# A hybrid decoder on one core: adaLN products one to a softmax step, and the softmax normalisation of five heads on ScalarE

## The chip, the cores and the metric

The kernel runs on one core of a Trainium2 chip. The metric is device time in microseconds (us) for one execution. The engines are named as in the profile: PE is TensorE's matmuls and PEld its weight loads, DVE is VectorE, ACT is ScalarE, POOL is GpSimd, and SP is the engine that issues most DMAs. A name followed by q (SPq) is the engine's instruction queue.

## The reference

The program is a two-layer decoder on 512 tokens of 1024 channels, all in float32. Layer 0 has attention, layer 1 a gated delta rule, and each has a SwiGLU FFN. What matters here is layer 0: a modulation vector computed from the condition `c`, and eight softmax heads ("moba") beside eight stick-breaking heads.

```python
cond = jax.nn.silu(c)
mod = (cond @ ada_w[layer] + ada_b[layer])          # 6 x 1024 numbers: six vectors
shift_m, scale_m, gate_m, shift_f, scale_f, gate_f = jnp.split(mod, 6, axis=-1)
h = rmsnorm(x, norm_mix_g) * (1 + scale_m) + shift_m
p = softmax(concat([s_sel, s_own]))                 # softmax heads; for 512 keys: causal
oa = p @ v                                          # then the stick-breaking heads, and
x = x + gate_m * (concat([oa, ob]) @ w_out)         # the output projection
h = rmsnorm(x, norm_ffn_g) * (1 + scale_f) + shift_f
x = x + gate_f * swiglu(h)
```

## The kernel before

Float32 accuracy is had by splitting each operand of a matmul into a high and a low part (`split`, L249 on ACT for the high part, L254 on DVE for the low part) and multiplying three times. Every engine runs its own instructions strictly in the order in which they stand in its queue; a scheduler with a cost model of its own makes these orders when the program is built, from the data dependencies and from `tc.issue_after`, which holds an instruction back until another one stands in the queue.

**The adaLN products.** Each of the 6 x 8 column blocks of the modulation needs the product of a 128x1024 block of `ada_w` with `cond`, summed along the row. `ada` (L206) issues a 512 KB DMA on SP's queue (L209) into the tile `aw` and then one DVE instruction (L214). The pool holds two `aw` tiles, so the third DMA can start only when the first product is done. The first two of the six vectors are needed before attention and are computed there; the last is left to the FFN. The 24 products of vectors 2, 3 and 4 fall in the attention stage.

**The softmax heads.** The heads run in four pairs; `moba` does one softmax head in four steps of 128 queries (i = 0 to 3) with 128 to 512 keys each, followed by `stick` for a stick-breaking head. A step is a chain: PE makes the scores `s` in a single PSUM bank (L744 to L747), DVE takes the row maximum (L759), ACT the exponential with its row sum (L761), DVE the reciprocal of the sum (L762) and the product of `p` with it (L763, "normalisation"), PE transposes `p` (L767), ACT and DVE split the result. Between these chains the scheduler places the `stick` work (`z`, `u`, `ssh`, `ssl`, `sq`) and the projections of the next pair (`mm` <- `hh`, `wh`), so that PE always has something.

**Where the 24 products stand.** `ADA = (0, 6, 6, 6, 6, 0, 0, 0)` puts six of them behind the reciprocal of the last step of each of the second to fifth heads (L814 to L817). In the output projection, `between` would take those left over, which are none.

The weights of the output projection (`raw` <- attn_out) are loaded on SP's queue (L292) between and behind these DMAs, and then the residual `x` (L153).

Of the kernel before, what the change touches and what calls it, by code (L numbers as in the profile page):

```python
# [12 lines left out]
AF = mybir.ActivationFunctionType  # L13
OP = mybir.AluOpType
# [53 lines left out]
OG, NG = (6, 8), 18  # L68
GS = 4
ROT = 2  # L70
AENG = "v"
ADA = (0, 6, 6, 6, 6, 0, 0, 0)
NSPLIT = 4
NFIRST = 2
NFIRST_GDN = 2
# [55 lines left out]
def build(nc, tc, I, O):  # L131
    V, G, A, PE = nc.vector, nc.gpsimd, nc.scalar, nc.tensor
    from contextlib import ExitStack
    ctx = ExitStack()
    with ctx:
# [38 lines left out]
        apool = actx.enter_context(tc.tile_pool(name="apool", bufs=1))  # L174
        cond = apool.tile([128, D], F32, name="cond")
# [27 lines left out]

        mod = const.tile([128, 96], F32, name="mod")

        def ada(layer, comp, chunk, pool=apool, bufs=2, eng="v"):  # L206
            j = layer * 48 + comp * 8 + chunk
            w = pool.tile([128, D], F32, name="aw", tag="aw", bufs=bufs)
            nc.sync.dma_start(w, I["ada_w"][j])  # L209
            if eng == "g":  # L210
                ins = G.tensor_tensor(w, w, cond, op=OP.mult)
                A.activation(w, w, AF.Copy, accum_out=mod[:, j:j + 1])
                return ins
            return V.tensor_tensor_reduce(w, w, cond, 1.0, 0.0, OP.mult, OP.add, mod[:, j:j + 1])  # L214

        fin = const.tile([128, 96], F32, name="fin")
# [318 lines left out]
def attention(e, x0ctx):  # L535
    nc, tc, V, G, A, PE, I = e.nc, e.tc, e.V, e.G, e.A, e.PE, e.I
    from contextlib import ExitStack
    with ExitStack() as ctx:
# [73 lines left out]
        with e.psum_pool("start") as sp:  # L612
            pq = [sp.tile([128, T], F32, name=f"pq{i}") if i < 1 else e.mm_tile() for i in range(4)]
            pv = [sp.tile([128, T], F32, name=f"pv{i}") for i in range(4)]
            with e.pool("rtmp") as tmp:
                for k in range(KC):
# [7 lines left out]
                    ins = e.norm_h(FULL, 0, 0, 1, hs, (k,))  # L624
# [3 lines left out]
                    a, z = k == 0, k == KC - 1  # L628
# [111 lines left out]
        def qk3(ps, k, ks, q, qs, at, mask):  # L740

            kh, kl = k
            qh, ql = q
            PE.matmul(ps, kh[:, ks], qh[:, qs], start=True, stop=False)  # L744
            PE.matmul(ps, kh[:, ks], ql[:, qs], start=False, stop=False)
            PE.matmul(ps[:, at], e.identb, mask, start=False, stop=False)
            steps[-1].append(PE.matmul(ps, kl[:, ks], qh[:, qs], start=False, stop=True).ins)  # L747

        def moba(pair, h, q, k):

            ph = work.tile([128, 1920], F32R, name="ph", tag="ph", bufs=1)
            pl = work.tile([128, 1920], F32R, name="pl", tag="pl", bufs=1)
            for i in range(4):
                n = 128 * (i + 1)
                qs = slice(i * 128, n)
                s = psum.tile([128, T], F32, name="s", tag="s", bufs=1)
                qk3(s[:, :n], q[h], qs, k, slice(0, n), qs, causal)
                st = work.tile([128, 3], F32, name="st", tag="st", bufs=4)
                V.tensor_reduce(st[:, 0:1], s[:, :n], AX.X, OP.max, negate=True)  # L759
                p = work.tile([128, T], F32, name="p", tag="p", bufs=2)  # L760
                A.activation(p[:, :n], s[:, :n], AF.Exp, bias=st[:, 0:1], accum_out=st[:, 1:2])  # L761
                ins = V.reciprocal(st[:, 2:3], st[:, 1:2])  # L762
                V.tensor_scalar(p[:, :n], p[:, :n], st[:, 2:3], None, op0=OP.mult)  # L763
                pt = psum.tile([128, T], F32, name="pt", tag="pt", bufs=1)
                for j in range(i + 1):
                    js = slice(j * 128, j * 128 + 128)
                    PE.transpose(pt[:, js], p[:, js], e.ident)  # L767
                src = pt[:, :n].rearrange("p (j q) -> p j q", q=128)
                e.split(src, *(x[:, i * 128:i * 128 + 384 * (i + 1)].rearrange("p (j q) -> p j q", q=384)[:, :, :128]
                               for x in (ph, pl)))  # L770
            pv_out(pair, h * 64, "m", ph, pl, lambda x, j: x[:, 512 * j:512 * j + 512 - 128 * j])
            return ins

        def stick(pair, h, q, k):
            off = {3: 0, 2: 128, 1: 384, 0: 768}
# [34 lines left out]
        for p in range(4):  # L810
            qa, ka, qb, kb = cur
            for h in range(2):
                steps.append([])
                ins = moba(p, h, qa, ka)  # L814
                for j in range(sum(ADA[:2 * p + h]), sum(ADA[:2 * p + h + 1])):
                    with tc.issue_after(ins.ins):
                        e.ada(0, 2 + j // 8, j % 8, eng=AENG[j % len(AENG)])  # L817
                stick(p, h, qb, kb)
            if p == 0:
                vproj(1)  # L820
            if p < 3:
                spread(32, 2 * p, 2 * p + 2)
                cur = [proj(p + 1, i) for i in range(4)]
# [4 lines left out]
        e.open_keep()  # L828

        def between(n, ins):  # L830
            a = sum(ADA)
            m = (24 - a) // 4
            for j in range(a + n * m, a + n * m + m):
                with tc.issue_after(ins.ins):
                    e.ada(0, 2 + j // 8, j % 8)
            if n == 3:
                e.ada_fin(0, 3)
                e.ada_fin(0, 4, gain=e.gffn[:, 0:8])
# [479 lines left out]
```

## Time and profile before

| | |
|---|---|
| median of three runs | 1441.11 us (1438.31 to 1442.24) |
| the profiled execution | 1445.06 us, of it 1443.2 us span |
| PE busy | 1390.6 us, 96% |
| DVE busy | 831.2 us, 58% |
| ACT busy | 580.3 us, 40% |
| chain that ended last | PE 80%, DVE 8%, DMA 6%, ACT 3% |
| costliest group on DVE beside the weight splits | L214, 96 products, 124.1 us |

"Busy" is the time in which an engine had an instruction running; the granted clock is the share of TensorE's full clock. A time in the trace counts from the start of the span. The attention stage with its eight heads lies between about 85 and 300 us.

### The profile page before, as it was taken

How to read it: one execution, taken by the hardware profiler on the slowest of the kernel's cores; microseconds unless marked ns; L12 is line 12 of the kernel's file. 1: busy time of each engine (PE TensorE's matmuls, PEld its weight loads, DVE VectorE, ACT ScalarE, POOL GpSimd, SP SyncE). 2: the span in 40 equal slices, each digit the busy share in tenths (PEclk: the TensorE clock that was granted, in tenths of full speed). 3: DMA queues.
4: the chain of work that ended last, by engine and by line, in shares of the span. 5: the costliest groups of instructions: out<-in, count | busy, mean ns of one | idle time of the engine just before them, and what ended most of it. 6: DMA issues, size and time to landing. Idle time of an engine off the chain costs nothing.

```text
span 1443.2 us, 19371 instructions
## 1 busy us (share of the span) xinstructions
PE 1390.6 (96%) x7418; PEld 1172.9 (81%) x7418; DVE 831.2 (58%) x1410; ACT 580.3 (40%) x1114; POOL 337.4 (23%) x336
## 2 busy tenths in 40 slices
PE   7999898999999999999899989999999999999997
PEld 4787677889888888888878877888998888888887
DVE  6776778646566566423777897436783333333233
ACT  4465565745222222222446743336662222222222
POOL 5023342213111111010424734311031111110010
PEclk8999999999999999999999999999999999999999
DMA  9437664042476666444522314312361332333332
GB/s 369 150 77 181 181 178 129 30 146 89 147 234 225 231 227 216 150 127 124 182 73 74 88 61 130 102 60 88 115 207 45 102 101 90 102 94 92 92 103 74
DMA packets 58734, 190.66 MB, mean 132 GB/s; under 512 B 7081, under 2 KB 11305, under 8 KB 58642
## 3 DMA queue, kind: packets, MB, share of 16 engines
q1 hardware_dynamic: 53376, 173.56, 37.1%
q0 software_dynamic: 4112, 14.82, 4.6%
q8 instruction: 58, 0.95, 0.3%
q10 hardware_dynamic: 1154, 1.05, 0.2%
q14 instruction: 34, 0.28, 0.1%
HBM read 184.11 MB, written 5.29 MB: 131 GB/s over the span
## 4 chain that ended last, share of the span: by engine, by line
PE 80%; DVE 8%; DMA 6%; ACT 3%; POOL 2%; issue 1%; SPq 0%; DVEq 0%; ACTq 0%; POOLq 0%
PE mm L332 20%; PE mm L333 20%; PE mm L335 20%; DMA aw<-in_ada_w_dram 3%; DVE aw L214 1%; PE mm L1126 1%; PE mm L1124 1%; PE mm L1125 1%; PE f L335 1%; PE bank L958 1%; DVE DT L1018 1%; DVE wl L254 1%; PE f L333 1%; PE f L332 1%; DMA call<-in_consts_dram 1%
## 5 line engine op out<-in xcount | busy, mean ns | idle before, releaser
L249 ACT ACTIVATE wh<-raw 128x1024 fp32r<-128x1024 f32 (+1 forms) x199 | 206.9, 1040 | 536.2 <-PE mm L333 493.1
L254 DVE TENSOR_TENSOR wl<-raw,wh 128x1024 fp32r<-128x1024 f32 (+1 forms) x193 | 234.1, 1214 | 195.7 <-ACT wh L249 175.4
L332 PE MATMUL mm<-hh,wh 128*128 128x512 f32 (+1 forms) x776 | 292.4, 381 | 0.2
L333 PE MATMUL mm<-hl,wh 128*128 128x512 f32 (+1 forms) x776 | 291.5, 379 | 0.0
L335 PE MATMUL mm<-hh,wl 128*128 128x512 f32 (+1 forms) x776 | 246.3, 378 | 0.4 <-DVE wl L254 0.4
L333 PEld LDWEIGHTS mm<-hl,wh 128*128 128x128 f32 x776 | 147.0, 190 | 27.6
L332 PEld LDWEIGHTS mm<-hh,wh 128*128 128x128 f32 x776 | 146.9, 190 | 26.9 <-ACT wh L249 0.3
L335 PEld LDWEIGHTS mm<-hh,wl 128*128 128x128 f32 x776 | 142.6, 189 | 29.4 <-DVE wl L254 0.6
L214 DVE CUSTOM_DVE_ANT_0 aw<-aw,cond 128x1024 f32<-128x1024 f32 x96 | 124.1, 1314 | 18.6 <-DMA aw<-in_ada_w_dram 18.5
L251 POOL TENSOR_SCALAR ah<-ac 128x512 fp32r<-128x512 f32 x36 | 53.3, 1481 | 330.4 <-DVE ac L496 330.4
L333 PE MATMUL mm<-al,wh 128*128 128x512 f32 (+1 forms) x354 | 124.6, 356 | 0.0
L332 PE MATMUL mm<-h1h,wh 128*128 128x512 f32 x320 | 124.5, 389 | 0.0
L333 PE MATMUL mm<-h1l,wh 128*128 128x512 f32 x320 | 124.5, 389 | 0.0
L332 PE MATMUL mm<-ah,wh 128*128 128x512 f32 (+1 forms) x354 | 124.2, 356 | 0.1
L496 DVE TENSOR_TENSOR ac<-sg,mm 128x512 f32<-128x512 f32 x40 | 27.5, 687 | 151.5 <-PE mm L335 151.5
L335 PE MATMUL mm<-h1h,wl 128*128 128x512 f32 x320 | 105.0, 389 | 0.0
L335 PE MATMUL mm<-ah,wl 128*128 128x512 f32 (+1 forms) x354 | 104.2, 356 | 0.0
L332 PEld LDWEIGHTS mm<-ah,wh 128*128 128x128 f32 x354 | 66.7, 189 | 9.7 <-ACT ah L249 0.4
L333 PEld LDWEIGHTS mm<-al,wh 128*128 128x128 f32 x354 | 66.8, 189 | 9.6
L335 PEld LDWEIGHTS mm<-ah,wl 128*128 128x128 f32 x354 | 64.2, 189 | 9.6 <-DVE wl L254 0.2
L335 PEld LDWEIGHTS mm<-h1h,wl 128*128 128x128 f32 x320 | 60.1, 188 | 12.5
L333 PEld LDWEIGHTS mm<-h1l,wh 128*128 128x128 f32 x320 | 60.1, 188 | 12.4
(403 smaller groups left out, 2557.7 us busy)
## 6 DMA issues: line engine op xcount, KB each, us to landing
aw<-in_ada_w_dram SPq DMA_DIRECT2D x96, 512.0 KB
raw<-in_ffn_in_dram SPq DMA_DIRECT2D x88, 512.0 KB
raw<-in_ffn_out_dram SPq DMA_DIRECT2D x36, 512.0 KB
raw<-in_gdn_in_dram SPq DMA_DIRECT2D x26, 512.0 KB
raw<-in_gdn_z_dram SPq DMA_DIRECT2D x16, 512.0 KB
raw<-in_gdn_out_dram SPq DMA_DIRECT2D x16, 512.0 KB
raw<-in_ffn_out_dram SPq DMA_DIRECT2D x18, 384.0 KB
wh<-in_attn_in_dram POOLq DMA_DIRECT2D x12, 512.0 KB, 4.1
```

Source lines behind the costliest of these rows:

```text
L214: return V.tensor_tensor_reduce(w, w, cond, 1.0, 0.0, OP.mult, OP.add, mod[:, j:j + 1])
L249: ins = A.activation(h, src, AF.Copy)
L251: G.tensor_scalar(h, src, 1.0, 1.0, op0=OP.mult, op1=OP.mult)
L254: (G if eng == "p" else V).tensor_tensor(l, src, h.bitcast(F32), op=OP.subtract)
L332: PE.matmul(ps, wh[k][:, 0], xh[:, cs], start=first and i == 0, stop=False)
L333: PE.matmul(ps, wh[k][:, 0], xl[:, cs], start=False, stop=False)
L335: PE.matmul(ps, wl[j][:, 0], x[j][0][:, cs], start=False, stop=last and j == order[-1])
L496: ins = V.tensor_tensor(ac, sg, pu, op=OP.mult)
L958: PE.matmul(ps[:, c], lhs[:, cs], rhs[:, cs], start=True, stop=True)
L1018: V.tensor_tensor(d, DS[:, :m, m:m + 1].to_broadcast([128, m, w]), DV[:, m:m + 1, m:].to_broadcast([128, m, w]), op=OP.mult)
L1124: PE.matmul(p, xh[:, t], wh[:, k - j], start=k == 0, stop=False)
L1125: PE.matmul(p, xl[:, t], wh[:, k - j], start=False, stop=False)
```

## The change

The 24 products are no longer put in six behind a head's last step. Instead one is issued behind the reciprocal of every step, from the first step of the second head (`ADA0 = 4`) to the last step of the seventh. For the second to the sixth head (`NACT = (1, 6)`, counted from 0) the normalisation of `p` becomes an ACT instruction, a copy with a scale read per row; the first, seventh and eighth heads keep it on DVE. A branch of `ada` that no call used is gone.

```diff
-AENG = "v"
-ADA = (0, 6, 6, 6, 6, 0, 0, 0)
+ADA0 = 4
+NACT = (1, 6)
...
                 ins = V.reciprocal(st[:, 2:3], st[:, 1:2])
-                V.tensor_scalar(p[:, :n], p[:, :n], st[:, 2:3], None, op0=OP.mult)
+                step = 4 * (2 * pair + h) + i - ADA0
+                if 0 <= step < 24:
+                    with tc.issue_after(ins.ins):
+                        e.ada(0, 2 + step // 8, step % 8)
+                if NACT[0] <= 2 * pair + h < NACT[1]:
+                    A.activation(p[:, :n], p[:, :n], AF.Copy, scale=st[:, 2:3])
+                else:
+                    V.tensor_scalar(p[:, :n], p[:, :n], st[:, 2:3], None, op0=OP.mult)
...
-                ins = moba(p, h, qa, ka)
-                for j in range(sum(ADA[:2 * p + h]), sum(ADA[:2 * p + h + 1])):
-                    with tc.issue_after(ins.ins):
-                        e.ada(0, 2 + j // 8, j % 8, eng=AENG[j % len(AENG)])
+                moba(p, h, qa, ka)
...
         def between(n, ins):
-            a = sum(ADA)
-            m = (24 - a) // 4
-            for j in range(a + n * m, a + n * m + m):
-                with tc.issue_after(ins.ins):
-                    e.ada(0, 2 + j // 8, j % 8)
             if n == 3:
```

DVE's queue before, at the last step of the fourth head (`ISA aw,mod` is a product and `ISA mod` reads its sum; `bl`, `pl`, `ssl` are low parts; line numbers are those of the kernel that is shown):

```order
L762 RECIPROCAL st<-st 128x1
L214 ISA aw,mod<-aw,cond 128x1024
L214 ISA mod 128x1
L214 ISA aw,mod<-aw,cond 128x1024
L214 ISA mod 128x1
L763 TENSOR_SCALAR p<-p,st 128x512
L254 TENSOR_TENSOR ssl<-u,ssh 128x256
```

The same place of DVE's queue in the changed kernel, whose line numbers are 4 lower here:

```order
L758 RECIPROCAL st<-st 128x1
L210 ISA aw,mod<-aw,cond 128x1024
L210 ISA mod 128x1
L795 SCALAR_TENSOR_TENSOR u<-z,u 128x256
L250 TENSOR_TENSOR ssl<-u,ssh 128x256
L250 TENSOR_TENSOR bl_189<-o,bh_188 64x512
```

One product stands behind the reciprocal in place of two, and the normalisation has left DVE's queue.

ACT's queue before, at the third and fourth step of the third head (`p,st<-s,st` is the exponential):

```order
L761 ACTIVATE p,st<-s,st 128x384
L249 ACTIVATE ph<-pt 128x2x128
L249 ACTIVATE bh-1_186<-o 64x512
L801 ACTIVATE sq<-z 128x128
L801 ACTIVATE sq<-z 128x256
L761 ACTIVATE p,st<-s,st 128x512
L249 ACTIVATE ph<-pt 128x3x128
```

The same place of ACT's queue in the changed kernel:

```order
L757 ACTIVATE p,st<-s,st 128x384
L764 ACTIVATE p<-p,st 128x384
L245 ACTIVATE bh-1_186<-o 64x512
L245 ACTIVATE ph<-pt 128x2x128
L803 ACTIVATE sq<-z 128x128
L803 ACTIVATE sq<-z 128x256
L757 ACTIVATE p,st<-s,st 128x512
L764 ACTIVATE p<-p,st 128x512
```

The normalisation stands directly behind the exponential whose row sum DVE must invert in between, and the rest of ACT's queue stands behind it.

SP's queue before, behind the loads of the value projection's weights:

```order
L209 DMA aw<-in_ada_w_dram 128x1024 x18
L292 DMA raw<-in_attn_out_dram 128x1024
L209 DMA aw<-in_ada_w_dram 128x1024 x6
L292 DMA raw<-in_attn_out_dram 128x1024 x4
L153 DMA x_2975<-in_x_dram 128x512
```

And in the changed kernel:

```order
L209 DMA aw<-in_ada_w_dram 128x1024 x15
L288 DMA raw<-in_attn_out_dram 128x1024
L209 DMA aw<-in_ada_w_dram 128x1024 x4
L288 DMA raw<-in_attn_out_dram 128x1024 x2
L209 DMA aw<-in_ada_w_dram 128x1024 x2
L288 DMA raw<-in_attn_out_dram 128x1024
L209 DMA aw<-in_ada_w_dram 128x1024
L288 DMA raw<-in_attn_out_dram 128x1024
L209 DMA aw<-in_ada_w_dram 128x1024 x2
L153 DMA x_2975<-in_x_dram 128x512
```

The loads of the output projection's weights now stand in among the product DMAs of the fifth to seventh heads. (Two of the 24 product DMAs are issued earlier in the queue, and the last two here are the FFN's.)

## Rows read from the trace of the kernel before

**Rows 1.** Stretches of the attention stage (line one names the columns)

```profile
core 0: us, PE busy (x) PEld busy (x) DVE busy (x) ACT busy (x) POOL busy (x), PEclk, DMA share, GB/s
125.00:235.00 110.00, 99.39 (x515) 80.02 (x514) 87.75 (x177) 64.56 (x149) 40.16 (x47) 0.95 0.71 196
235.00:290.00 55.00, 51.63 (x299) 43.28 (x298) 37.76 (x79) 39.48 (x101) 15.44 (x20) 0.97 0.11 37
```

**Rows 2.** Timeline of PE: start, length, instruction [idle before, what ended it]

```profile
144.35 0.38 PE L744 MATMUL s<-kah,qah 128*128 128x256 f32 x1 [2.01 <-ACT p L761]
...
147.23 0.30 PE L767 MATMUL pt<-call,p 128*128 128x128 f32 x1 [0.81 <-DVE p L763]
...
177.77 0.79 PE L799 MATMUL z<-ssl,ntri 128*128 128x512 f32 x1 [3.18 <-DVE ssl L254]
...
179.57 0.79 PE L744 MATMUL s<-kah,qah 128*128 128x512 f32 x1 [0.72 <-ACT p L761]
...
207.81 0.73 PE L799 MATMUL z<-ssl,ntri 128*128 128x512 f32 x1 [1.99 <-DVE ssl L254]
...
241.72 0.33 PE L744 MATMUL s<-kah,qah 128*128 128x128 f32 x1 [2.32 <-ACT p L761]
```

**Rows 3.** Timeline of DVE at three of the waits for a product's data

```profile
142.37 1.22 DVE L214 CUSTOM_DVE_ANT_0 aw<-aw,cond 128x1024 f32<-128x1024 f32 x1 [4.06 <-DMA aw<-in_ada_w_dram]
...
175.28 1.22 DVE L214 CUSTOM_DVE_ANT_0 aw<-aw,cond 128x1024 f32<-128x1024 f32 x1 [2.90 <-DMA aw<-in_ada_w_dram]
...
205.45 1.23 DVE L214 CUSTOM_DVE_ANT_0 aw<-aw,cond 128x1024 f32<-128x1024 f32 x1 [1.45 <-DMA aw<-in_ada_w_dram]
```

**Rows 4.** PE in the three stretches at half clock (PE busy, granted clock, DMA)

```profile
177.20:184.00 6.80, 5.51 (x13) 0.50 0.50 158
207.90:211.30 3.40, 3.40 (x9) 0.50 0.88 205
242.08:245.44 3.36, 3.36 (x12) 0.50 0.51 156
```

**Rows 5.** DVE's groups by shape, 104 to 244.6 us (busy, mean ns | idle before)

```profile
L214 DVE CUSTOM_DVE_ANT_0 aw<-aw,cond 128x1024 f32<-128x1024 f32 x24 | 29.6, 1244 | 13.2 <-DMA aw<-in_ada_w_dram 13.2
...
L763 DVE TENSOR_SCALAR p<-p,st 128x512 f32<-128x512 f32 x5 | 3.9, 778 | 0.0
...
L763 DVE TENSOR_SCALAR p<-p,st 128x384 f32<-128x384 f32 x5 | 3.1, 615 | 0.1
L763 DVE TENSOR_SCALAR p<-p,st 128x256 f32<-128x256 f32 x5 | 2.9, 584 | 0.1
...
L763 DVE TENSOR_SCALAR p<-p,st 128x128 f32<-128x128 f32 x5 | 2.7, 531 | 0.0
```

**Rows 6.** Line 763 over the same stretch: ns min/median/max, first and last start

```profile
L763 DVE TENSOR_SCALAR p<-p,st x20: 267/480/1589, 106.4 to 242.9; 128x128 f32<-128x128 f32 x5, 128x256 f32<-128x256 f32 x5, 128x384 f32<-128x384 f32 x5, 128x512 f32<-128x512 f32 x5
```

**Rows 7.** ACT's groups by shape, the same stretch: the exponential

```profile
L761 ACT ACTIVATE p<-s,st 128x512 f32<-128x512 f32 x5 | 3.4, 686 | 1.1 <-DVE st L759 1.0
...
L761 ACT ACTIVATE p<-s,st 128x384 f32<-128x384 f32 x5 | 2.9, 574 | 1.4 <-DVE st L759 1.3
...
L761 ACT ACTIVATE p<-s,st 128x256 f32<-128x256 f32 x5 | 2.3, 466 | 0.0
...
L761 ACT ACTIVATE p<-s,st 128x128 f32<-128x128 f32 x5 | 1.8, 358 | 5.6 <-DVE st L759 5.6
```

**Rows 8.** ACT's waits, 90 to 320 us: total us, times, longest

```profile
ACT ssh L249 <- DVE u L793: 20.1, 15, 6.9
ACT p L761 <- DVE st L759: 7.9, 5, 5.2
```

**Rows 9.** The chain of waits, 60 to 340 us: start, length, its longest DMA

```profile
135.14 10.49 DMA aw<-in_ada_w_dram
```

**Rows 10.** Timelines of SP's queue and of ACT at the output weights

```profile
232.30 28.22 SPq L292 DMA_DIRECT2D raw<-in_attn_out_dram  x4
...
236.83 1.06 ACT L249 ACTIVATE wh<-raw 128x1024 fp32r<-128x1024 f32 x1 [1.24 <-DMA raw<-in_attn_out_dram]
```

More of the change, by code (lines that the diff above doesn't have):

```diff
@@ L204, in build, with ada @@
         mod = const.tile([128, 96], F32, name="mod")
-        def ada(layer, comp, chunk, pool=apool, bufs=2, eng="v"):
+        def ada(layer, comp, chunk, pool=apool, bufs=2):
             j = layer * 48 + comp * 8 + chunk
@@ L209, in ada @@
             nc.sync.dma_start(w, I["ada_w"][j])
[L210 to L213, printed above, removed]
             return V.tensor_tensor_reduce(w, w, cond, 1.0, 0.0, OP.mult, OP.add, mod[:, j:j + 1])
@@ L771, in moba @@
             pv_out(pair, h * 64, "m", ph, pl, lambda x, j: x[:, 512 * j:512 * j + 512 - 128 * j])
-            return ins
         def stick(pair, h, q, k):
```

## The prediction

> **What bounds the kernel now.** I read the page's busy shares first (PE 96%: the kernel is as long as PE's stream of matmuls and the holes in it), then stretches of the attention stage, where the change is, then PE's holes one by one with what ended each, then the queues of DVE and ACT behind them.
>
> The stretch 125 to 235 us holds nearly all of the 24 products before. In its 110 us PE is idle 110 - 99.39 = 10.61 us, and DVE is busy 87.75 us (80%) [rows 1]. DVE has 13.2 us more in which a product at the head of its queue waited for its DMA [rows 5]; so 101 of 110 us are taken, and what stands behind a late product is late by the whole wait. The three largest waits but one show it: 4.06 us until 142.37, 2.90 until 175.28, 1.45 until 205.45 [rows 3], and PE's holes follow: 2.01 us until 144.35 (it wants the score bank, which the exponential frees, which wants the maximum behind the product), 3.18 until 177.77 and 1.99 until 207.81 (it wants the low part `ssl`, two or three instructions behind the product), 0.72 until 179.57 and 0.81 until 147.23 in the wake of these or of the next late product [rows 2]. Sum: 8.71 us.
>
> Two of these holes cost a second time. The granted clock is 0.50, the lower of TensorE's two levels (1.2 of 2.4 GHz), from 177.2 to 184.0 us and from 207.9 to 211.3 us, each time right after a hole; PE worked 5.51 and 3.40 us in them, and half of that, 2.76 + 1.70 = 4.46 us, is lost [rows 4].
>
> Why the data are late is in the order: six products stand within one head, often two in a row, and with two `aw` tiles the third DMA starts only when the first product is done. The longest landing on the chain is 10.49 us [rows 9].
>
> **The change, part by part.** Sums are made in the profiled execution, 1445.06 us; it lies 4 us above the median of the runs, 1441.11, and I subtract the result from the median.
>
> *One product per step.* The products themselves are kept, 24 of 1244 ns on DVE [rows 5]; they are only spread. A product's DMA still starts when the product two before it ends, but that is now two steps. Twenty normalisations, one to a step, start between 106.4 and 242.9 us [rows 6]: 136.5 / 19 = 7.2 us a step, and 6.4 us if some 14 us go. Two steps less one product are 2 x 6.4 - 1.24 = 11.6 us, more than 10.49 [rows 9]. So most of the 13.2 us of waiting goes, and with it 8.71 + 4.46 = 13.17 us of PE. Steps are not even: in the new order some reciprocals of the fourth and fifth heads follow each other with two or three instructions between, so a DMA can still be late there. Bounds for what stays: 0 and 13.17 us. The row nearest to it is the shortest of the three waits shown, 1.45 us [rows 3], and I take 1.5.
>
> *Eight products move into the sixth and seventh heads.* There, from 235 to 290 us, DVE is busy 37.76 of 55 us [rows 1]. Eight products add 8 x 1.244 = 9.95 us: 47.7 us, 87 to 90% of the stretch, while only the sixth head loses its normalisation. The fill is that of 125 to 235 us now (101 of 110), where the holes not due to late data are 10.61 - 8.71 = 1.90 us in 110 [rows 1, 2]: half of that for half the length, 1 us. In the seventh head the product stands between the reciprocal and the normalisation, so it lies on the step's own chain; four times 1.244 us, 5 us, is the upper bound, nothing the lower (the projections of the next pair and `stick` cover it). I take 1.5 us. If the cover is gone, a drop of the clock as at 242.08 us adds 3.36 / 2 = 1.7 us [rows 4].
>
> *Normalisation on ACT.* DVE loses 20 instructions of 3.9 + 3.1 + 2.9 + 2.7 = 12.6 us [rows 5]. They run from 267 to 1589 ns [rows 6], so a part of that is waiting at the start of the instruction. ACT has not run a copy with a scale per row here; the nearest rows are the exponentials of the same four shapes, with an operand per row: 686 + 574 + 466 + 358 = 2084 ns per head, 10.4 us in five heads [rows 7]. Lengths therefore change little. In 125 to 235 us ACT's busy time goes from 64.56 to about 73 us (16 of the 20 fall there) in a stretch of some 96 us, 76%; DVE's goes from 87.75 to 87.75 - 9.95 - 10.1 = 67.7 us, 71%.
>
> The Trainium skill speaks against this part: ScalarE: Activation LUTs, Rules for kernel authors, gives multiplications to VectorE and not to ScalarE. Against the shortest of the rows here (267 ns for 128 columns) it holds; against the means that this kernel has (531 to 778 ns) it does not. If DVE would run all 20 undisturbed, the part would lengthen each step's chain, by my estimate about 3 us over the five heads, and the sum below would give 1432.5 in place of 1429.5.
>
> What the part adds is a wait: the exponential on ACT, the reciprocal on DVE, the normalisation on ACT again. In the new order it often stands directly behind the exponential, and then everything in ACT's queue (`ph` and `sq`, which PE wants, and `ssh`) stands still until DVE has come to the reciprocal. Bounds: nothing, where ACT has other work between (its idle share is above 20%); and 20 x 20.1 / 15 = 26.8 us, if each costs what ACT's dearest wait for DVE costs on average [rows 8]. The nearest row is ACT's wait for the maximum, the same kind of hop in the same chain: 7.9 us over 31 steps, 0.25 each, 5 us for 20 [rows 8], on ACT; a third of it reaching PE gives 1.5 us.
>
> *The other holes.* Left are 1.90 us in 125 to 235 us and the 2.32 us until 241.72 [rows 2] with its half clock, 3.36 / 2 = 1.68 us [rows 4]: 5.90 us, from a DVE that is behind and from ACT waiting 1.24 us for an output weight at 236.83 [rows 10]. An emptier DVE should return the first kind; the second may stay, since on SP's queue that second weight now stands behind four product DMAs more than the first, and so leaves only when the third step of the sixth head is done. I count half, 2.95 us.
>
> *Queue of SP and the rest.* The residual's loads stand behind the last two product DMAs, which leave when the seventh head's last products are done, a whole head ahead of the end; before, SP was in the row of output weights, which begins at 232.30 and lasts 28.22 us [rows 10], so nothing is late for them. Some small projections at the start of the delta rule change places among larger matmuls that hide them; I cost that at nothing.
>
> Sum: -13.17 - 2.95 + 1.5 + 1.5 + 1.5 = -11.6 us. 1441.1 - 11.6 = **1429.5 us**.
>
> **Rivals.**
> *Late data stay.* Steps bunch, DMAs of weights and products overlap (DMA share 0.71 in 125 to 235 us, 0.88 in the second half-clock stretch [rows 1, 4]), and half of the 13.17 us stays: -6.6 - 2.95 + 3 = -6.5, 1434.5 us. For it: the landing of 10.49 us leaves only 1 us of margin on the mean step. Against: one DMA is on its way at most times in place of two.
> *ACT becomes the queue that PE waits for* (slower). At each of the 20 steps ACT stands still behind the reciprocal. At 1.34 us a step on PE's path it costs 26.8 us against 13.17 + 2.95 returned: 1441.1 + 26.8 - 16.1 = 1452 us. It decides from 16.1 / 20 = 0.8 us a step. For it: the order puts nothing between exponential and normalisation at about half of the steps, and the first wait in rows 8 shows how long ACT can stand for DVE. Against: the reciprocal stands ahead of its product in DVE's queue, and DVE is then a quarter idle.
> *The holes only move.* PE's next wait, for the chain within a step, takes the place of the late data: 1441 us. For it: PE is busy 99.39 of 110 us already. Against: from 235 to 290 us, with no products at all, PE was idle 55 - 51.63 = 3.37 us, 2.32 of it at the start [rows 1, 2], so the chains alone do not hold it.
> *Everything returns.* 13.17 + 5.90 = 19.1 us: 1422 us.
>
> **How the numbers follow.** Forecast (7 to 17 us back) 0.55; late data 0.15; holes move 0.12; ACT's queue 0.11; all of it 0.07. A difference of 0.3%, 4.3 us, is about what a measurement of this kernel tells from none. Faster by more: 0.53 + 0.07 + 0.13 + 0.02 = 0.75; within: 0.02 + 0.02 + 0.08 + 0.01 = 0.13; slower: 0.02 + 0.10 = 0.12. The range for 8 in 10 goes from a little below the case in which all returns to the case in which the holes move: 1421 to 1441.
>
> **What would show it.** Right: DVE's wait for `aw` falls from 13.2 to under 4 us; PE's holes behind `ssl` and the score bank between 125 and 235 us shrink to some 2 us; at most one half-clock stretch is left there; the stretch to 290 us is not over 3 us longer for its eight products. Wrong: the `aw` waits stay above 6 us (late data); ACT waits for the reciprocal for more than 10 us and PE's holes end on ACT's normalisation or on `ph` (ACT's queue); or PE's holes between 100 and 290 us still sum to 13 us or more with other releasers (they move).

## The result, and the profile after

| | before | changed |
|---|---|---|
| median | 1439.9 us (1438.31 to 1442.24, 4 runs) | 1429.7 us (1427.02 to 1430.3, 4 runs) |
| profiled execution, span | 1445.06, 1443.2 us | 1427.02, 1425.2 us |
| PE busy | 1390.6 us | 1380.8 us |
| DVE, ACT busy | 831.2, 580.3 us | 819.4, 589.5 us |
| chain that ended last | PE 80%, DVE 8%, DMA 6% | PE 83%, DVE 7%, DMA 4% |

The ratio is 0.9914, 95% interval [0.9896, 0.9932]. The forecast was 1429.5 us.

To compare whole stages I use two marks that every version of the kernel has: PE's first hole of the stage (a matmul `mm` <- `wh`, `hh` that waits for the low part `bl`, near 80 us) and its last (`mm` <- `bh`, `wh` that waits for `bh`, 280 to 300 us). I call what lies between **the stage**. PE does the same 1132 or 1133 recorded matmuls in it in all of them. These are some of PE's holes in the changed kernel, the largest up to 260 us among them; its line numbers are 4 lower in helpers such as `split`, and the first and the last row are the marks.

```profile
78.76 0.36 PE L718 MATMUL mm<-wh,hh 128*128 128x256 f32 x1 [1.68 <-DVE bl L250]
...
144.64 0.38 PE L740 MATMUL z<-qbh,kbh 128*128 128x256 f32 x1 [1.28 <-ACT sq L803]
...
223.78 0.33 PE L801 MATMUL z<-ssh,ntri 128*128 128x128 f32 x1 [0.75 <-ACT ssh L245]
...
280.24 0.73 PE L328 MATMUL mm<-bh,wh 128*128 128x512 f32 x2 [0.68 <-ACT bh L245]
```

Where [rows 2] had six holes of 0.7 to 3.2 us, 11.03 us in all, the largest one between the first mark and 260 us is now 1.28 us. The stage took 297.81 - 81.28 = 216.53 us before and takes 280.24 - 78.76 = 201.48 us now. Two stretches of the kernel before, the stage and its last part (columns as in [rows 1]):

```profile
81.28:297.81 216.53, 200.34 (x1132) 166.41 (x1133) 154.62 (x327) 136.36 (x329) 70.05 (x85) 0.97 0.47 127
...
240.00:298.00 58.00, 53.10 (x304) 44.22 (x305) 36.08 (x78) 40.90 (x103) 12.64 (x18) 0.97 0.09 28
```

The stretches of the changed kernel, the stage first, its last part second:

```profile
78.76:280.24 201.48, 193.76 (x1133) 162.69 (x1133) 145.74 (x307) 145.13 (x349) 70.25 (x85) 1.00 0.51 136
...
225.00:281.00 56.00, 52.00 (x302) 42.33 (x300) 40.25 (x84) 40.06 (x98) 15.20 (x18) 1.00 0.23 77
...
125.00:235.00 110.00, 105.89 (x586) 87.69 (x585) 84.82 (x166) 79.89 (x186) 43.37 (x50) 1.00 0.63 170
```

The granted clock of the stage is 1.00: the three half-clock stretches of [rows 4] have no counterpart. In 125 to 235 us PE is idle 4.11 us (10.61 in [rows 1], though the stage has moved on by some 15 us at its end, so that the later part is other work). The last part of the stage has 4.00 us of idle PE in 56 us, before it had 4.90 us in 58 us.

The 24 products on DVE wait for nothing now, against 13.2 us in [rows 5]:

```profile
L210 DVE CUSTOM_DVE_ANT_0 aw<-aw,cond 128x1024 f32<-128x1024 f32 x24 | 31.4, 1310 | 0.0
```

The normalisations on ACT, by shape (columns as in [rows 7]), in the changed kernel:

```profile
L764 ACT ACTIVATE p<-p,st 128x512 f32<-128x512 f32 x5 | 3.6, 722 | 0.4 <-DVE st L758 0.2
...
L764 ACT ACTIVATE p<-p,st 128x384 f32<-128x384 f32 x5 | 3.1, 616 | 0.7 <-DVE st L758 0.7
L764 ACT ACTIVATE p<-p,st 128x256 f32<-128x256 f32 x5 | 2.5, 509 | 0.6 <-DVE st L758 0.6
...
L764 ACT ACTIVATE p<-p,st 128x128 f32<-128x128 f32 x5 | 2.0, 406 | 0.1
```

And ACT's waits in it (total us, times, longest), which answer to [rows 8]:

```profile
ACT ssh L245 <- DVE u L795: 8.3, 11, 2.6
...
ACT p L757 <- DVE st L755: 5.2, 8, 1.0
...
ACT p L764 <- DVE st L758: 1.5, 6, 0.3
```

The copies run 36 to 48 ns longer than the exponentials of the same shape in [rows 7]. The added wait for the reciprocal is 1.5 us in six of 20 steps, never more than 0.3 us, and the wait of `ssh` for DVE fell from 20.1 to 8.3 us.

### The profile page after: what moved, and what is told of

It is laid out like the page before. It is cut to its first block, busy times and chain, and to the rows that moved or that the text cites. A ratio compares the mean times of both kernels' runs of the same rounds, so it can differ in the third digit from the quotient of the medians.

```text
span 1425.2 us, 19359 instructions
## 1 busy us (share of the span) xinstructions
PE 1380.8 (97%) x7418; PEld 1167.1 (82%) x7418; DVE 819.4 (57%) x1390; ACT 589.5 (41%) x1134; POOL 337.4 (24%) x336
## 4 chain that ended last, share of the span: by engine, by line
PE 83%; DVE 7%; DMA 4%; ACT 3%; issue 2%; POOL 2%; SPq 0%; DVEq 0%; ACTq 0%; POOLq 0%
PE mm L328 21%; PE mm L329 21%; PE mm L331 20%; DMA wh<-in_attn_in_dram 2%; PE z L801 1%; PE mm L1120 1%; PE mm L1118 1%; PE mm L1119 1%; PE f L331 1%; PE bank L952 1%; DVE DT L1012 1%; DVE wl L250 1%; PE f L329 1%; PE f L328 1%; DMA call<-in_consts_dram 1%
## 5 line engine op out<-in xcount | busy, mean ns | idle before, releaser
L250 POOL TENSOR_TENSOR wl<-raw,wh 128x1024 fp32r<-128x1024 f32 x24 | 58.5, 2438 | 52.2 <-ACT wh L245 52.0
L349 POOL TENSOR_TENSOR ssq<-ssq,sq 128x512 f32<-128x512 f32 x14 | 21.9, 1561 | 205.6 <-ACT sq L345 205.6
```

Source lines behind the costliest of these rows:

```text
L250: (G if eng == "p" else V).tensor_tensor(l, src, h.bitcast(F32), op=OP.subtract)
L349: eng.tensor_tensor(ssq[:, cs], ssq[:, cs], sq[:, cs], op=OP.add)
```

## The experiments

Two questions are open after this. The kernel before had late data, as the prediction said, but it also had six products within some 20 us of DVE's queue; which of the two made the holes? And did the ACT part do anything? All comparisons are with the kernel before, run beside them: 1440.37 us beside changed again, spread only, ACT only and no loads; 1440.58 us beside four per head, spread over four heads, one tile and no products; 1442.22 us beside the other four. Kernels of different groups are compared by their ratios.

Every edit changes more than it says: the scheduler makes the queues' orders anew for each kernel, and even around instructions that the edit leaves alone they are not the same. So one kernel alone proves little here, and the argument goes by several of each kind.

| kernel | products, loads, normalisation | median us | ratio | stage us | DVE's waits for `aw`, us |
|---|---|---|---|---|---|
| before again | six behind a head, all loads, DVE | 1441.07 | 0.9992 [0.9975, 1.0008] | 216.52 | 12.7 |
| changed again | one a step, ACT | 1432.55 | 0.9938 [0.9922, 0.9955] | 201.97 | 0 |
| spread only | one a step, DVE | 1429.35 | 0.9917 [0.9901, 0.9933] | 202.28 | 0 |
| ACT only | six behind a head, ACT | 1441.86 | 1.001 [0.9995, 1.0024] | 211.26 | 14.2 |
| no loads | six behind a head, one load, DVE | 1440.71 | 0.9999 [0.9988, 1.001] | 212.19 | 0 |
| four per head | four behind a head, six heads | 1435.91 | 0.9964 [0.995, 0.9979] | 209.24 | 2.0 |
| spread, four heads | one or two a step, old heads | 1438.45 | 0.9984 [0.9971, 0.9997] | 207.70 | 2.9 |
| one tile | one a step, a single `aw` tile | 1454.78 | 1.0097 [1.0075, 1.0118] | 212.82 | 9.2 |
| no products | none | 1429.67 | 0.9919 [0.9898, 0.9939] | 200.30 | none |
| ACT, no loads | six behind a head, one load, ACT | 1447.55 | 1.0031 [1.0015, 1.0046] | 220.61 | 0 |
| spread four, no loads | one or two a step, old heads, one load | 1426.37 | 0.9883 [0.9862, 0.9905] | 199.47 | 0 |
| four per head, no loads | four behind a head, one load | 1439.57 | 0.9978 [0.9965, 0.9991] | 211.21 | 0 |

The stage is read from one profile of each kernel, between the two marks. It is not the same measure as the median: ACT only and no loads have stages 4 to 5 us shorter than before and medians that are not. Both profiles of the kernel before are of executions above its medians (1445.06 and 1444.15 us), and that of ACT, no loads is of its slowest (1451.57 us). In the two profiles of the kernel before 1228.53 and 1227.63 us lie outside the stage; at a median of 1441 us the stage would then take some 213 us, by this estimate, and not 216.5. Whether a kernel is faster is read from the ratios, and the stage shows where in the program a difference arises.

### The change again

> The changed kernel once more, beside the kernel before on the same chip and beside the three kernels below. Late-data theory (the gain is that products no longer wait for their DMA at the head of VectorE's queue) and the rivals all expect the same here: 9 to 12 us less than before, ratio 0.991 to 0.994, and no wait of a product for its data.

Measured: 1432.55 us, stage 201.97 us. The gain is there in other runs, with 7.8 us a little under the 9 to 12 us expected; by the two measurements it is between 7.8 and 10.2 us.

### The two parts apart

Spread only: `NACT = (0, 0)` in the changed kernel.

```diff
-NACT = (1, 6)
+NACT = (0, 0)
```

> One product per step as in the change, all normalisations on VectorE as before. Late-data theory: most of the gain is there, 8 to 12 us less than before, and VectorE's wait for the product data is under 2 us. Rival (the gain comes from 12.6 us of normalisation leaving VectorE): 0 to 4 us less than before. Second rival (any new order of the queues would do): no expectation that tells this run from the next.

Measured: 1429.35 us, stage 202.28 us. ACT only is the kernel before, with six products behind a head and the normalisation of heads two to six on ACT:

```diff
+NACT = (1, 6)
...
-                V.tensor_scalar(p[:, :n], p[:, :n], st[:, 2:3], None, op0=OP.mult)
+                if NACT[0] <= 2 * pair + h < NACT[1]:
+                    A.activation(p[:, :n], p[:, :n], AF.Copy, scale=st[:, 2:3])
+                else:
+                    V.tensor_scalar(p[:, :n], p[:, :n], st[:, 2:3], None, op0=OP.mult)
```

> Normalisations of heads two to six on ScalarE as in the change, products six to a head as before. Late-data theory: the waits for product data stay at 9 us or more in sum and the time falls by 0 to 4 us; it may even rise by 1 to 2 us, since ScalarE stands behind a reciprocal that stands behind late products. Rival (VectorE relieved is what counts): 7 us or more less than before.

Measured: 1441.86 us. Its stage is 5 us shorter than in the profiles of the kernel before, but the runs show no gain. DVE's wait there (one row of the waits) is as it was:

```profile
DVE aw L215 <- DMA aw<-in_ada_w_dram: 14.2, 8, 4.7
```

So the spread carries the whole gain, and the ACT part gives none. With it the median is 1432.55 us, without it 1429.35. Beside each other the six runs of either hardly overlap (1430.05 to 1436.06 and 1427.66 to 1431.28 us), but the first four runs of the change lay at 1427.02 to 1430.3 us, and in the profiles the difference is not in the stage, where the ACT part stands: the stages agree within 0.3 us, and 1431.58 - 201.97 = 1229.61 against 1428.85 - 202.28 = 1226.57 us lie outside. Whether the part costs up to 3 us stays open.

### The products with their data always there

The kernel before, with its 24 products computed from a single block, so that it leaves out 23 loads and three of the modulation's vectors are not the program's:

```diff
...
+            if pool is apool and layer == 0 and comp < 5:
+                if not held:
+                    for i in range(2):
+                        held.append(pool.tile([128, D], F32, name="aw", tag="aw", bufs=bufs))
+                    nc.sync.dma_start(held[0], I["ada_w"][j])
+                return V.tensor_tensor_reduce(held[1], held[0], cond, 1.0, 0.0, OP.mult, OP.add, mod[:, j:j + 1])
```

> The kernel before with the 24 products of the attention stage six to a head, but all computed from one block that is loaded once: the loads of 23 blocks of the modulation weights are left out, so that no product can wait for data; their 12 MB leave the DMA queues too. Late-data theory: 9 to 14 us less than before, the TensorE holes behind late products gone, the half-clock stretches near 177 and 208 us too. Rival (VectorE relieved): VectorE does the same work in the same bursts, so 0 to 3 us less.

Measured: 1440.71 us, ratio 0.9999. This is the run against which my main step falls: no product waits for data, and nothing comes back in the runs. (The order changed too: around the fourth head the six products now stand singly, from 161.66 to 179.13 us; before, two of them stood in a row, from 158.13 to 179.22 us.) Its stretches: the stage, the 24 us around the fourth head's products, and a stretch at the lower clock.

```profile
80.57:292.76 212.19, 199.26 (x1132) 166.42 (x1133) 157.91 (x327) 136.43 (x329) 69.92 (x85) 0.98 0.32 75
...
158.00:182.00 24.00, 21.04 (x102) 17.16 (x102) 22.95 (x43) 13.50 (x32) 9.71 (x10) 0.87 0.39 87
...
176.20:183.00 6.80, 6.04 (x21) 5.01 (x21) 6.66 (x16) 1.67 (x6) 0.00 (x0) 0.53 0.01 2
```

DVE's timeline in those 24 us shows what is late in place of the data (`rq` and `rs` are the rotation of the next pair's projections):

```profile
164.43 1.21 DVE L215 CUSTOM_DVE_ANT_0 aw<-aw,cond 128x1024 f32<-128x1024 f32 x1
...
166.03 1.83 DVE L676 TENSOR_TENSOR rq<-rq,C 128x512 f32<-128x512 f32 x1
...
167.99 2.87 DVE L215 CUSTOM_DVE_ANT_0 aw<-aw,cond 128x1024 f32<-128x1024 f32 x1
...
170.79 1.24 DVE L248 TENSOR_TENSOR fin<-mod,cols 128x8 f32<-128x8 f32 x1
171.95 0.68 DVE L677 TENSOR_TENSOR rq<-rq,rs 128x512 f32<-128x512 f32 x1
172.56 0.15 DVE L770 RECIPROCAL st<-st 128x1 f32<-128x1 f32 x1
172.63 1.20 DVE L215 CUSTOM_DVE_ANT_0 aw<-aw,cond 128x1024 f32<-128x1024 f32 x1
```

ACT's timeline at the same place: `qah` waits for the `rq` that ended at 172.63, and `ssh` stands behind it.

```profile
172.67 0.63 ACT L257 ACTIVATE qah<-rq 64x512 fp32r<-64x512 f32 x1 [2.77 <-DVE rq L677]
...
174.07 0.31 ACT L257 ACTIVATE ssh<-u 128x128 fp32r<-128x128 f32 x1
```

And PE's hole that follows:

```profile
174.44 0.33 PE L807 MATMUL z<-ssh,ntri 128*128 128x128 f32 x1 [1.90 <-ACT ssh L257]
```

The hole of [rows 2] at 177.77 has its counterpart here: the data are ready, but the products and what comes with them still stand ahead of what ACT and PE want. PE waits 1.90 us in place of 3.18, and the lower clock follows again (0.53 on average over 6.8 us). A good part of this delay is stretching: a product of 2.87 us in place of 1.21, and a `fin` of 1.24 us that takes 0.15 us in the kernel before. So the rows show that something other than data holds up the queue; they don't show that it is the number of products.

### Smaller bunches, and a spread over the old heads

Four per head: one line of the kernel before.

```diff
-ADA = (0, 6, 6, 6, 6, 0, 0, 0)
+ADA = (0, 4, 4, 4, 4, 4, 4, 0)
```

> The kernel before with four products behind the last step of each of the second to seventh heads in place of six behind each of the second to fifth; normalisations on VectorE. Crowding theory (products that follow each other within a few steps fill VectorE, and TensorE waits for what stands behind them, late data or not): the bunches are smaller, 2 to 6 us less than before, clearly less gain than the 11 us of one product per step. Late-data theory: of each bunch all but the two loaded ahead are late, 12 in place of 16, so a quarter of the gain, 2 to 4 us. Load theory (what counts is the products per head, four and not six): the same gain as with one product per step, 9 to 12 us.

Measured: 1435.91 us, 4.7 us less than before. That is what the crowding theory expected, and a little more than the late-data theory; the load theory's 9 to 12 us are not there. Spread, four heads: the changed kernel with `NACT = (0, 0)` and one or two products behind each of the 16 steps of heads two to five.

```diff
-                if 0 <= step < 24:
-                    with tc.issue_after(ins.ins):
-                        e.ada(0, 2 + step // 8, step % 8)
+                for j in range((3 * step + 1) // 2, (3 * step + 4) // 2):
+                    if 0 <= j < 24:
+                        with tc.issue_after(ins.ins):
+                            e.ada(0, 2 + j // 8, j % 8)
```

> Products spread over the steps of the second to fifth heads alone, two and one in turn (six to a head as before); normalisations on VectorE. Crowding theory: 6 to 11 us less than before, since no more than two products stand together. Load theory: 0 to 4 us less, since each of these heads has as much VectorE work as before. Late-data theory: a product has 1.3 steps for its load in place of 2, so some waits come back (3 to 8 us in sum on VectorE), and the gain is 5 to 9 us.

Measured: 1438.45 us, 2.1 us less than before: the crowding theory and the late-data theory both expected more, and only the load theory's range holds it (the run without loads below speaks against that theory). In both kernels DVE's waits for the data fell from 13 us to 2 or 3 us, and only 2 to 5 us came back in the medians.

### Late data in the spread order

One tile: spread only, with a single `aw` tile, so that each DMA starts only when the product before it is done. It holds for the 24 products here and for the FFN's 56; the first 16, ahead of attention, keep tiles of their own.

```diff
-        def ada(layer, comp, chunk, pool=apool, bufs=2):
+        def ada(layer, comp, chunk, pool=apool, bufs=1):
```

> One product per step, normalisations on VectorE, but a single tile for the product data in the whole kernel, so that each load starts only when the product one step before is done. This puts late data back without bunching: with 6.4 us a step and 1.2 us for the product 5 us are left for a load that takes 4 to 10 us. Late-data theory: VectorE waits 20 us or more for the data in the attention stage, and at least half of it reaches the end: 0 to 10 us slower than before. Crowding theory: a late product also holds up what stands behind it, but there is room behind it to catch up within the step: VectorE waits as much, and less than a third of it reaches the end, so that this is still 2 to 8 us faster than before.

Measured: 1454.78 us, slower than either theory allowed. More than half of that arises in the FFN, which has one tile too: outside the stage the profiled execution is 1242.00 - 1226.57 = 15.43 us longer than that of spread only. In the stage alone, DVE waits

```profile
DVE aw L210 <- DMA aw<-in_ada_w_dram: 9.2, 10, 2.4
```

and the stage is 212.82 - 202.28 = 10.54 us longer than with two tiles. The waits are less than half of what was expected. In this order late data cost about as much as they last.

### No products at all

In the kernel before, a constant is written to the modulation in place of the 24 products:

```diff
-                    with tc.issue_after(ins.ins):
-                        e.ada(0, 2 + j // 8, j % 8, eng=AENG[j % len(AENG)])
+                    V.memset(e.mod[:, 16 + j:17 + j], 1.0)
```

> The kernel before without the 24 products and their loads in the attention stage (the modulation's vectors 2 to 4 are left out and set to one): what they cost at most. If the products are hidden once they stand one to a step: 10 to 13 us less than before, no better than 2 us below the kernel with one product per step. If they still cost something there: 15 us or more less than before.

Measured: 1429.67 us, ratio 0.9919, the same as spread only (0.9917): one to a step, the products cost nothing that the runs can tell. This is not a floor, though, for its order is a new one too, and it has a late spot of its own. A product of the rotation stretches on DVE, with no adaLN product near,

```profile
164.91 5.00 DVE L668 TENSOR_TENSOR rq<-rq,C 128x512 f32<-128x512 f32 x1
```

and PE has a hole behind it:

```profile
171.05 0.30 PE L767 MATMUL pt<-call,p 128*128 128x128 f32 x1 [1.96 <-DVE p L763]
```

### Bunch or late data, or VectorE too full

The last four kernels combine edits that are shown above: the single block in the order of ACT only, of the spread over four heads, and of four per head; and the kernel before once more.

> The kernel before with both suspected costs lowered at once: normalisation of heads two to six on ScalarE (about 10 us less on VectorE between 125 and 235 us), and the 24 products (six to a head, as before) computed from one block that is loaded once, the other 23 loads left out. Each of the two alone gave nothing (ratios 1.001 and 0.9999). Theory 'either cost is enough to make the holes' (late data, or VectorE full behind a bunch): with both lowered at least half of the 11 us returns, 1434 us or less, PE busy above 104 of 110 us from 125 to 235. Rival 'six products in one place hold up the chain by themselves, whatever the rest of the queue': six in a row are 7.5 us on VectorE at one step, nothing returns, 1438 us or more. Rival 'ScalarE's copy takes what VectorE gives': also 1438 or more, but with PE's holes ending on ScalarE.

Measured: 1447.55 us, slower than before. The theory that lowering both costs returns the time fell. That nothing returned is what the rival of the six products in one place expected. DVE's rows show one of these products and ahead of it an `rq` that took 4.03 us in place of 0.68:

```profile
166.58 0.56 DVE L249 TENSOR_TENSOR fin<-mod,cols 128x8 f32<-128x8 f32 x1
167.06 0.28 DVE L768 TENSOR_REDUCE st<-s 128x1 f32<-128x128 f32 x1
167.27 4.03 DVE L678 TENSOR_TENSOR rq<-rq,rs 128x512 f32<-128x512 f32 x1
171.22 1.21 DVE L216 CUSTOM_DVE_ANT_0 aw<-aw,cond 128x1024 f32<-128x1024 f32 x1
172.36 0.08 DVE L216 DVE_READ_ACCUMULATOR2_ANT mod<- 128x1 f32 x1
172.36 0.15 DVE L771 RECIPROCAL st<-st 128x1 f32<-128x1 f32 x1
```

ACT's row of that moment waits 3.29 us for it, and `ph`, which PE wants, is next:

```profile
171.33 0.63 ACT L258 ACTIVATE qah<-rq 64x512 fp32r<-64x512 f32 x1 [3.29 <-DVE rq L678]
171.86 0.57 ACT L258 ACTIVATE ph<-pt 128x512 fp32r<-128x512 f32 x1
```

PE has a hole of 2.30 us behind that `ph`. Why this version is slower than no loads alone (1.0031 against 0.9999) is not settled; ACT's queue also waits for the reciprocal there, up to 3.1 us at once, so that in this order the ACT part may cost something.

> One or two products a step in heads two to five, normalisation on VectorE, 23 of the 24 loads left out. With its loads this order took 1438.45 us (0.9984). Theory 'VectorE has too much to do in these four heads': the same without loads, 1436 to 1440 us, VectorE above 90 of 110 us. Rival 'data still late with two products at a step': 1433 us or less.

Measured: 1426.37 us, ratio 0.9883, the fastest of all (it does less loading). The theory that these four heads give VectorE too much to do fell, and clearly: here are its stage and the 24 us that were shown of no loads.

```profile
80.96:280.43 199.47, 194.04 (x1132) 163.46 (x1132) 154.17 (x327) 135.37 (x329) 71.21 (x85) 0.99 0.35 80
...
158.00:182.00 24.00, 22.24 (x119) 17.86 (x119) 22.47 (x46) 15.78 (x39) 10.28 (x11) 1.00 0.40 89
```

DVE is as full (22.47 of 24 us against 22.95), with six products in either stretch and no load to wait for, and PE is busy 22.24 us in place of 21.04, at a clock of 1.00 in place of 0.87. The edits differ only in where the products stand, behind each step of the four heads or behind the last step: 0.9883 against 0.9999, with intervals far apart. Fill and number do not tell the two apart, nor do long products: two of the six here are long as well (2.25 and 1.95 us). What does is ACT's wait for the rotation's `rq`, 9.1 us over the stage in no loads and 0.6 us here (total us, times, longest):

```profile
ACT kah L257 <- DVE rq L677: 4.9, 3, 3.4
ACT qah L257 <- DVE rq L677: 4.2, 2, 2.8
```

```profile
ACT kah L253 <- DVE rq L673: 0.4, 1, 0.4
ACT qah L253 <- DVE rq L673: 0.2, 1, 0.2
```

It is 2.6 to 5.3 us in the other kernels with four or six products behind a head, 0.7 to 1.3 us with one to a step and two `aw` tiles or with none, and 1.7 to 2.0 us with one tile and in the spread over four heads with its loads. So behind a head's last step the products seem to stand in the way of the next pair's rotation; no run moved them away from it alone. In the spread order with its loads the stage was 207.70 us with 2.9 us of waits; so there it is the loads that cost, and by more than those waits. What the rest is, traffic or the new order, I did not separate.

> Four products behind the last step of each of heads two to seven, 23 of the 24 loads left out. With its loads this order took 1435.91 us (0.9964). Theory 'the bunch itself holds up the chain': four in one place are 5 us on VectorE, and the time stays at 1434 to 1437 us. Rival 'late data make the rest of the difference to one per step': 1431 us or less, as one per step (1429.35).

Measured: 1439.57 us, 2 to 3 us above what the bunch theory gave, and far from one per step. By the ratios, leaving out the loads gained nothing here (0.9978 against 0.9964 with them, intervals that overlap). Without loads, bunches of four and of six have stages of 211.21 and 212.19 us, against 199.47 us spread. So without late data the cost in the stage does not follow the number of products in the bunch.

> The kernel before, unchanged, for what a difference of nothing looks like in these comparisons, and for a second profile of its attention stage. The ratio should hold 1 within 0.15%; the stage should again take 210 us or more from the first projection of the heads to the last, with TensorE's holes of over 1.5 us behind low parts, maxima or exponentials near the six products of a head, and one to three stretches at half clock. If the second profile's stage took 205 us or less, the comparison of single profiles would be worth little.

Measured: 1441.07 us, ratio 0.9992. Some of PE's holes in this second profile of the kernel before, with the two marks:

```profile
80.29 0.36 PE L722 MATMUL mm<-wh,hh 128*128 128x256 f32 x1 [1.68 <-DVE bl L254]
...
143.09 0.38 PE L744 MATMUL s<-kah,qah 128*128 128x256 f32 x1 [1.44 <-ACT p L761]
...
175.55 0.49 PE L799 MATMUL z<-ssl,ntri 128*128 128x512 f32 x1 [2.17 <-DVE ssl L254]
...
206.49 0.61 PE L799 MATMUL z<-ssl,ntri 128*128 128x512 f32 x1 [2.41 <-DVE ssl L254]
...
240.86 0.48 PE L744 MATMUL s<-kah,qah 128*128 128x128 f32 x1 [2.29 <-ACT p L761]
...
296.81 0.50 PE L332 MATMUL mm<-bh,wh 128*128 128x512 f32 x1 [0.68 <-ACT bh L249]
```

They are the holes of [rows 2], 0.9 to 2.2 us earlier, and the stage is the same to 0.01 us (216.52 and 216.53). The two profiles of the changed kernel agree to 0.49 us (201.48 and 201.97) though their executions are 4.56 us apart. A difference of 10 us between stages is far above that. One of 4 to 5 us between the kernel before and another bunched kernel says little, since neither profile of the kernel before is of an execution near its median.

## Why the prediction was right or wrong

**The size.** Forecast -11.6 us; the medians fell by 10.2 us at first and by 7.8 us again. The profiles fell by more, 1445.06 - 1427.02 = 18.04 us, of it 216.53 - 201.48 = 15.05 us in the stage. Of these, PE's idle time gives (216.53 - 200.34) - (201.48 - 193.76) = 16.19 - 7.72 = 8.47 us and PE's busy time, which the lower clock had lengthened, 200.34 - 193.76 = 6.58 us; the prediction had 8.71 and 4.46 us for these, and 2.95 us for the other holes. The profiles fell by more than the medians because they lie at opposite ends: that of the kernel before 1445.06 - 1439.9 = 5.16 us above its median, that of the changed kernel 1429.7 - 1427.02 = 2.68 us below. So the close match of 8.47 and 6.58 us with the terms is a match with an execution that is longer than most.

**One product per step: the number held, its cause did not.** The step that failed is "So most of the 13.2 us of waiting goes, and with it 8.71 + 4.46 = 13.17 us of PE." The waiting went, all of it, and even where the working would not have it: twelve of the 22 gaps between a product and the next but one are shorter than the 10.49 us that I took for a load, the shortest (from 146.01 + 1.74 = 147.75 to 153.87 us) is 6.1 us. But "with it" is wrong. No loads, four per head and the spread over four heads each take away some 10 us or more of the waiting; by the medians 0, 4.7 and 2.1 us come back, and no loads still has 12.93 us of idle PE in its stage (212.19 - 199.26). The trace of the kernel before had a sign of it, in the one large wait that I left out. DVE waited 2.23 us there, and PE was busy 9.81 of the 10 us around it (columns as in [rows 1]):

```profile
198.46 1.23 DVE L214 CUSTOM_DVE_ANT_0 aw<-aw,cond 128x1024 f32<-128x1024 f32 x1 [2.23 <-DMA aw<-in_ada_w_dram]
```

```profile
196.00:206.00 10.00, 9.81 (x55) 8.12 (x53) 6.32 (x13) 6.14 (x13) 3.19 (x4) 1.00 0.77 243
```

I had read the holes of [rows 2] from the releaser of DVE's queue only: the product that waited stood first in the queue, so I gave its data the whole delay. With the data there, other work stands ahead of the same low parts and maxima: the products, up to six within some 20 us, and their neighbours, which stretch. The kernel before had both faults, late data and the bunched order. Each alone makes a stage of about 212 us (bunched without loads 212.19 and 211.21, spread with late data 212.82), neither makes 199 to 202 us, and both together made 216.5 in executions of 1444 to 1445 us, some 213 by the estimate above; so the two costs do not add up. One product per step mends both at once. That the sum came out is luck: the price of both faults had been read off one of them. What in the bunched order holds PE is open. It is not late data alone, and without loads four products cost as much as six; ACT's waits for `rq` point to their place behind a head's last step, and stretched instructions ahead of what is wanted may have a part in it. Also open is what loads cost in the order spread over four heads, 0.9984 with them and 0.9883 without, where only 2.9 us are waits.

**Other holes, 2.95 us.** The 2.32 us hole at 241.72 [rows 2] and its lower clock have no counterpart in the changed kernel, and the idle time left in the stage is 7.72 us; without any products it is 200.30 - 194.06 = 6.24 us. The term can't be told from the others by any run.

**Eight products in the sixth and seventh heads, +1.5 us.** Too careful: the last part of the stage is not longer (4.00 us of idle PE from 225 to 281 us, 58 - 53.10 = 4.90 us in the same part before), and the clock stays at 1.00.

**Normalisation on ACT, +1.5 us.** The wait for the reciprocal is 1.5 us in all on ACT's queue, under a third of the 5 us that I took from the wait for the maximum, and at most 0.3 us at once: the reciprocal comes first on DVE. Against it stand 12.6 us less on DVE that buy nothing either: by ACT only (1.001) and spread only (0.9917) the part gives no gain. (Of the 20 normalisations 15, not 16, start between 125 and 235 us; nothing in the sum hangs on that.)

The Trainium skill, ScalarE: Activation LUTs, Rules for kernel authors, gives multiplications to VectorE. That it is no gain to leave VectorE agrees with the runs. The loss of 3 us that the prediction worked out beside it, 1432.5 us, is not shown: the second measurement of the change is 1432.55 us and spread only is 1429.35 us, as it would be, but the first is 1429.7 us, and the two stages are 201.97 and 202.28 us.

**The rivals.** Late data did not stay (no wait). ACT did not become the queue that PE waits for: 1.5 us of waiting where that rival needed 16. The holes did not move: 7.72 us of idle PE remain of 16.19. All of it returning, 1422 us, was not reached by any kernel; the nearest is the spread over four heads without loads, 1426.37 us.

## What to carry to other kernels

A wait at the head of a queue says what is late now, not what would be late next: before its whole length is counted as gain, look at what the queue would do with the data there, and at a wait of the same kind that cost nothing. Here work that nobody needs soon was hidden by being put in single pieces between the steps of a chain, with its load started two pieces ahead; the same pieces behind a head's last step cost 12 us of a 200 us stage with the engine equally full and all data there. Moving 12.6 us of work off DVE, 71% busy in the stage, gave nothing, though PE's holes stood behind its queue; what helped was another order in that queue.

## What the runs showed of the hardware

DVE's instructions stretch by much more than I had counted: a product of 1.21 us took 2.87 us, and elementwise products of 0.68 and 0.69 us took 4.03 and 5.00 us in the rows above. In no loads, GpSimd's timeline at the long product is full of its own elementwise work:

```profile
167.84 1.35 POOL L814 TENSOR_TENSOR spl<-sq,sph 128x384 fp32r<-128x384 f32 x1
168.83 0.94 POOL L813 TENSOR_SCALAR sph<-sq 128x512 fp32r<-128x512 f32 x1
169.86 2.15 POOL L814 TENSOR_TENSOR spl<-sq,sph 128x512 fp32r<-128x512 f32 x1
```

The Trainium skill, SBUF — State Buffer, Who interferes with whom, says that a VectorE instruction with two inputs in SBUF contends with a GpSimd instruction that reads SBUF, and the rows agree: the long product and the `rq` products have two inputs in SBUF and stand beside such instructions. The products' own lengths do not explain the difference between the orders: in the spread order without loads the 24 took 1393 ns on average, in the bunched one 1365 ns. But the stage's 327 DVE instructions were busy 154.17 us in the spread order and 157.91 us in the bunched one, so a part of the 12.72 us between the stages may be stretching. That was not tested.

The times of whole executions of the kernel before spread from 1435.03 to 1448.29 us, while the two profiles of its stage, of executions of 1445.06 and 1444.15 us, agree to 0.01 us.
